# The input projection of a two-layer encoder as seven block products

## The chip, the cores and the metric

The kernel runs on one core of one Trainium2 chip. The time is device microseconds of one execution. Engines are named as in the profile: PE is TensorE's matmul (PEld its weight load), DVE is VectorE, ACT is ScalarE, POOL is GpSimd, SP is SyncE, which here only issues DMAs. Every row of a trace is from one execution.

## The reference

Two layers on 512 tokens of width 1024, all in float32. What one layer computes, cut to its core:

```python
h = rms_norm(x, g_pre_mix)
z = h @ w_in                      # 1024 x 6656
q, k, v, cb, cc, cx, ga, gb = split(z)   # 1024,256,256,1024,1024,1024,1024,1024
q, k = partial_rope(q), partial_rope(k)  # first 16 of 64 numbers of each head
y_attn = band_attention(q, k, v, sink) @ w_attn_proj   # |i-j| <= 128, 16 heads, 4 kv heads
y_conv = (cb * short_conv(cc * cx, conv_w)) @ w_conv_proj   # 3 taps
mix = (sigmoid(ga) * y_attn + sigmoid(gb) * y_conv) @ w_out
x = x + rms_norm(mix, g_post_mix)
h = rms_norm(x, g_pre_ffn)
x = x + rms_norm((silu(h @ w_gate) * (h @ w_up)) @ w_down, g_post_ffn)   # width 2816
```

## The kernel before

**Float32 from three products.** Every operand of a large matmul is kept as two parts: `h`, rounded to the matmul's format, and `lo`, the rest. ACT makes the first by a cast, DVE the second by a subtraction (`split_w` for weights, lines 129 to 131, and `split_to` for tokens, 205 to 207). A product is then three matmuls (`mm3`, lines 174 to 177): high times low, low times high, high times high, all into one PSUM bank.

**Stages of a layer.** (1) The norm, a transpose of the tokens by PE, and the value and key tiles. (2) The stretch with attention: a generator `products` yields the matmuls of the query tiles, of the conv's three column groups and of the conv projection, one k-block of three matmuls at a time, and pieces of attention (scores, softmax, transposed weights, values) are laid between them at even distances. (3) For each of eight column tiles the two gate products, their sigmoids, the attention projection and the merge. (4) `down` for `w_out`: all blocks but the last five first go through, the last five are kept in SBUF and finish the four token blocks one after the other, with the norms behind each. (5) The FFN's gate and up products. (6) `down` for `w_down`, six blocks kept.

In stages 1 to 3 the moving operand is the transposed tokens, 512 wide (256 for the keys), and a column tile of 128 takes 8 k-blocks of three matmuls.

**Stage 5 works by seven block products already.** `Rights` holds the token side: the 512 tokens and the 1024 rows form a 2 x 2 of blocks, and seven operands of 4 k-blocks by 256 tokens are made of them by sums and differences. `Pair` holds the weight side, two column tiles, one of the gate and one of the up matrix, as the other 2 x 2. Its `prep` makes the left operand of one product (a sum of blocks where needed, then the split), its `product` runs 12 matmuls of 256 columns and combines results on DVE. So a pair takes 7 x 12 matmuls of 256 columns. `orders` writes the order of the products by hand: five pairs open with products 2 and 1, which need the first 256 tokens alone, and later two pairs are in work at a time. Left operands are made five products ahead (`AHEAD`), loads begin ten ahead.

**What sets the order.** Every engine runs its own queue in order. The queues are filled by the framework's scheduler, which starts from the order of the code and moves instructions by its own estimate of when their inputs are there. Buffers: 22 units of 4 KB per partition (`u4`), six `t4`, six `t2`, eight `hl` (split weights), three `raw` (loaded weights); a tile waits until a buffer of its kind is free. Weight loads, stores of the layer's result and all other large DMAs are issued by SP.

**POOL** has little: the power -1/2 of the norms, two memsets per conv tile, and in the FFN one product of 256 columns per pair (line 448).

## Time and profile before

| | us |
|---|---|
| median of 3 runs | 1673.93 (1673.88 to 1674.6) |
| the profiled execution | 1674.66, its span 1672.9 |
| layer 0: start, values, keys | 0 to 39.6 |
| attention with query, conv products and conv projection | 39.6 to 314.3 |
| gates, attention projection, merge | 314.3 to 444.9 |
| `w_out` with norms | 444.9 to 489.0 |
| FFN products | 489.0 to 720.8 |
| `w_down` with norms | 720.8 to 838.0 |
| layer 1 and the end | 838.0 to 1672.9 |

A row of a group reads: line, engine, operation, what it writes and reads by the program's names, shapes and count, then busy microseconds, mean nanoseconds of one, and the idle time of the engine just before it with what ended it. A row of a timeline begins with start and duration. A row of a stretch (from:to) has its length and then, engine by engine, busy microseconds and in brackets the count. Busy PE time can hold matmuls that overlap, so the distance between starts is what a matmul costs.

### The profile page before, as it was taken

Reading aid. Unit: us, or ns where it says so; the run is one execution under the profiler, and the core shown is the slowest. Engines: PE = TensorE matmul, PEld = TensorE weight load, DVE = VectorE, ACT = ScalarE, POOL = GpSimd, SP = SyncE. Lnnn points to the kernel's source line nnn. Section 1 sums busy time; section 2 is a strip of 40 time slices with the busy share of each in tenths; the row PEclk is TensorE's granted clock in tenths of the full one; section 3 lists DMA queues with packets and bytes.
Section 4 is the critical chain, followed back from the end, with each engine's and each line's share of the span. In section 5 each row is a group of like instructions: output and inputs, shape, how many; then the busy total and the mean of one; then the engine's idle time right before and its main releaser. Section 6 shows DMA issues by size and latency. Waiting matters only on the chain.

```text
span 1672.9 us, 24896 instructions
## 1 busy us (share of the span) xinstructions
PE 1650.1 (99%) x9457; PEld 1454.9 (87%) x9457; DVE 1141.8 (68%) x2230; ACT 862.7 (52%) x1806; POOL 72.3 (4%) x114
## 2 busy tenths in 40 slices
PE   7999999999999999999999999999999999999998
PEld 7888888888889999988898888888888899999886
DVE  6988876434469988854469788754434899888442
ACT  5566666433346655543346666564333555556331
POOL 0000000000011100000000000000000011001000
PEclk9999999999999999999999999999999999999999
DMA  6322222433452333343413222224335333434332
GB/s 201 94 76 76 65 87 64 133 95 101 129 161 76 102 102 101 115 138 127 150 64 101 76 76 76 76 76 126 101 100 164 101 92 99 108 103 133 111 115 76
DMA packets 246937, 174.35 MB, mean 104 GB/s; under 512 B 5488, under 2 KB 232864, under 8 KB 246816
## 3 DMA queue, kind: packets, MB, share of 16 engines
q1 hardware_dynamic: 246096, 171.18, 34.6%
q8 instruction: 74, 1.21, 0.3%
q10 hardware_dynamic: 720, 1.57, 0.3%
q14 instruction: 47, 0.39, 0.1%
HBM read 164.34 MB, written 8.39 MB: 103 GB/s over the span
## 4 chain that ended last, share of the span: by engine, by line
PE 97%; DVE 2%; ACT 1%; DMA 0%; POOL 0%; issue 0%; POOLq 0%; DVEq 0%; ACTq 0%
PE bank L176 30%; PE bank L177 30%; PE bank L175 30%; PE bank L627 2%; PE bank L674 2%; PE bank L661 2%; PE bank L244 0%; DVE u L207 0%; DVE h L207 0%; DMA t<-in_x_dram 0%; ACT t L228 0%; PE bank L327 0%; DVE t L264 0%; POOL r L222 0%; DVE t L236 0%
## 5 line engine op out<-in xcount | busy, mean ns | idle before, releaser
L175 PE MATMUL bank<-h,hl 128*128 128x256 f32 (+1 forms) x1536 | 521.6, 340 | 1.1 <-DVE h L207 1.1
L176 PE MATMUL bank<-h,hl 128*128 128x256 f32 (+1 forms) x1536 | 518.2, 337 | 0.0
L177 PE MATMUL bank<-h,hl 128*128 128x256 f32 (+1 forms) x1536 | 517.8, 337 | 0.0
L131 DVE TENSOR_TENSOR hl<-raw,hl 128x512 fp32r<-128x512 f32 x428 | 292.8, 693 | 230.9 <-ACT hl L130 228.3
L130 ACT CAST hl<-raw 128x512 fp32r<-128x512 f32 x428 | 261.6, 620 | 323.4 <-PE bank L177 241.5
L177 PEld LDWEIGHTS bank<-h,hl 128*128 128x128 f32 x1536 | 292.2, 190 | 30.9
L175 PEld LDWEIGHTS bank<-h,hl 128*128 128x128 f32 x1536 | 292.5, 190 | 29.3 <-DVE h L207 1.9
L176 PEld LDWEIGHTS bank<-h,hl 128*128 128x128 f32 x1536 | 292.5, 190 | 27.6
L175 PE MATMUL bank<-u,hl 128*128 128x256 f32 (+1 forms) x784 | 251.2, 321 | 3.4 <-DVE u L207 3.4
L176 PE MATMUL bank<-u,hl 128*128 128x256 f32 (+1 forms) x784 | 250.2, 319 | 2.7 <-ACT u L206 1.8
L177 PE MATMUL bank<-u,hl 128*128 128x256 f32 (+1 forms) x784 | 250.0, 319 | 0.0
L175 PEld LDWEIGHTS bank<-u,hl 128*128 128x128 f32 x784 | 149.7, 191 | 13.8 <-DVE u L207 3.8
L176 PEld LDWEIGHTS bank<-u,hl 128*128 128x128 f32 x784 | 149.9, 191 | 13.0 <-ACT u L206 2.2
L177 PEld LDWEIGHTS bank<-u,hl 128*128 128x128 f32 x784 | 150.0, 191 | 10.3
L130 ACT CAST hl<-t 128x512 fp32r<-128x512 f32 x176 | 108.3, 621 | 58.2 <-DVE t L393 41.1
L131 DVE TENSOR_TENSOR hl<-t,hl 128x512 fp32r<-128x512 f32 x176 | 133.4, 765 | 6.0 <-ACT hl L130 3.9
L175 PE MATMUL bank<-hl,u 128*128 128x512 f32 x304 | 118.3, 389 | 0.0
L176 PE MATMUL bank<-hl,u 128*128 128x512 f32 x304 | 118.3, 389 | 0.0
L177 PE MATMUL bank<-hl,u 128*128 128x512 f32 x304 | 118.3, 389 | 0.0
L647 ACT ACTIVATE t<-t,neg 128x256 f32<-128x256 f32 (+1 forms) x128 | 70.4, 552 | 21.1 <-DVE neg L642 20.8
L632 DVE CUSTOM_DVE_ANT_0 t<-bank,tab,sink 128x256 f32<-128x256 f32 (+1 forms) x128 | 65.7, 541 | 6.1 <-PE bank L627 5.9
L448 POOL TENSOR_TENSOR u<-t 128x256 f32<-128x256 f32 x44 | 51.9, 1179 | 397.4 <-DVE t L444 236.6
(123 smaller groups left out, 2121.4 us busy)
## 6 DMA issues: line engine op xcount, KB each, us to landing
raw<-in_w_in_dram SPq DMA_DIRECT2D x104, 512.0 KB, 3.9
u<-in_w_up_dram SPq DMA_DIRECT2D x44, 512.0 KB, 5.9
raw<-in_w_down_dram SPq DMA_DIRECT2D x44, 512.0 KB, 3.5
raw<-in_w_gate_dram SPq DMA_DIRECT2D x40, 512.0 KB, 4.0
raw<-in_w_conv_proj_dram SPq DMA_DIRECT2D x16, 512.0 KB, 4.2
raw<-in_w_attn_proj_dram SPq DMA_DIRECT2D x16, 512.0 KB, 4.3
raw<-in_w_out_dram SPq DMA_DIRECT2D x16, 512.0 KB, 3.5
xd<-t SPq DMA_DIRECT2D x12, 512.0 KB, 2.9
```

The source lines that it names most:

```text
L130: nc.scalar.copy(h, raw)
L131: eng.tensor_tensor(out=lo, in0=raw, in1=h.bitcast(F32), op=ALU.subtract)
L175: nc.tensor.matmul(acc, wh, xl, start=first, stop=False, skip_group_check=goes_on)
L176: nc.tensor.matmul(acc, wl, xh, start=False, stop=False, skip_group_check=goes_on)
L177: nc.tensor.matmul(acc, wh, xh, start=False, stop=last, skip_group_check=goes_on)
L448: nc.gpsimd.tensor_tensor(out=out[:, TH:], in0=c22, in1=self.g[:, TH:], op=ALU.mult)
L627: nc.tensor.matmul(s[:, :w], q, kk[g][:, 1 - part, lo_b * P : lo_b * P + w], start=part == 0, stop=part == 1)
L632: nc.vector.tensor_tensor_reduce(out=p, in0=s[:, :w], in1=mask[:, m0 : m0 + w], scale=HD**-0.5, scalar=sink[:, h : h + 1], op0=ALU.add, op ...
L647: nc.scalar.activation(p, p, AF.Exp, bias=neg[:, i : i + 1], accum_out=den[:, i : i + 1])
L661: nc.tensor.transpose(pt[:, i * P : (i + 1) * P], p[:, n * P : (n + 1) * P], ident)
L674: nc.tensor.matmul(o, v, hl[:, 1 - part], start=n == 0 and part == 0, stop=kb == hi_b and part == 1)
```

## The change

**The input projection moves to `Pair`.** All columns but the values (50 tiles of a layer) become 25 pairs: one of keys, four of queries, eight of the conv (its X with its C columns), four of two B tiles each, eight of the two gates of one output tile. `orders` now also orders these, with four pairs opened early, and `products` yields them between the pieces of attention. The gate products move there from stage 3. Value tiles stay plain, with the tokens read from `Rights`; two of the four come after the transposes of the later tokens.

**A product's matmuls stand in another order:** for each k-block high times low and high times high, then all four low times high. Attention pieces can now stand between k-blocks of a product.

**More work on POOL.** `need` makes the two weight sums of a pair there, `rope` the sine product and the sum, the conv its product and the sum of two taps (the second tap's scaling goes to ACT), `Outer` the product with B, `sums` the token sums, the merge its gate product. In the FFN too the pair's two sums come from POOL, and DVE keeps two sums of four.

**DMA.** Rotated keys and queries are split whole and then moved to the two partition halves by DMAs (`move`), where ACT and DVE wrote the halves before. The conv results go to DRAM (`cyd`) and come back for the conv projection, the gates go to DRAM (`sgd`) and come back for the merge.

**Other edits.** Softmax by two heads instead of four, its scaling split evenly between ACT and DVE; attention's output kept in float32 and split behind the attention; units 22 to 20, `hl` 8 to 6, `t2` 6 to 8; separate buffers for scores; `down` keeps four blocks where it kept five and six; the next layer's first weights are loaded and split within `w_down`.

PE, where the products stand. Before, one k-block after another of 512 columns (`h` is the tokens, `hl` the split weights):

```order
L627 MATMUL bank_1405<-u_3_445,u_10_841 128x384 x2
L175 MATMUL bank_1364<-h_86,hl_1361 128x512
L176 MATMUL bank_1364<-h_86,hl_1361 128x512
L177 MATMUL bank_1364<-h_86,hl_1361 128x512
L175 MATMUL bank_1364<-h_86,hl_1361 128x512
L176 MATMUL bank_1364<-h_86,hl_1361 128x512
```

Of the change, one product:

```order
L421 MATMUL bank_1847<-h_95,hl_1780 128x256 x4
L417 MATMUL bank_1783<-h_95,hl_1811 128x256
L418 MATMUL bank_1783<-h_95,hl_1811 128x256
L417 MATMUL bank_1783<-h_95,hl_1811 128x256
L418 MATMUL bank_1783<-h_95,hl_1811 128x256
L417 MATMUL bank_1783<-h_95,hl_1811 128x256
L418 MATMUL bank_1783<-h_95,hl_1811 128x256
L417 MATMUL bank_1783<-h_95,hl_1811 128x256
L418 MATMUL bank_1783<-h_95,hl_1811 128x256
L421 MATMUL bank_1783<-h_95,hl_1811 128x256 x4
```

The tile's 24 matmuls of 512 columns became products of 12 matmuls of 256.

DVE, in the attention stretch of layer 0. Before (L131 is the split of a weight, L632 scores, L642 to L656 softmax, L207 the split of the transposed weights of attention, L606 of a query half):

```order
L650 TENSOR_TENSOR rd_2042<-den_2036,es_2034 128x4
L651 RECIPROCAL rd_2042<-rd_2042 128x4
L656 TENSOR_SCALAR t_43_1982<-t_43_1982,rd_2042 128x384
L656 TENSOR_SCALAR t_45_2023<-t_45_2023,rd_2042 128x384
L207 TENSOR_TENSOR t_46_2098<-bank_2093,t_46_2098 128x512
L606 TENSOR_TENSOR u_18_2058<-t_53_2052,u_18_2058 64x512 x2
L632 ISA t_47_2122,m_2121<-bank_2123,tab,sink 128x384
```

Of the change (L135 is the split of a weight, L397 a weight sum, L427, L433 and L446 combine products, L733 to L741 softmax, L204 the split for attention):

```order
L427 TENSOR_TENSOR t_33_2273<-bank_2216,t_33_2273 128x256
L733 TENSOR_TENSOR es_2247<-sink,neg_2246 128x2
L135 TENSOR_TENSOR hl_2293<-u_38_1889,hl_2293 128x512
L433 TENSOR_TENSOR t_30_2071<-bank_2137,t_30_2071 128x256
L135 TENSOR_TENSOR hl_2309<-raw_2151,hl_2309 128x512
L738 TENSOR_TENSOR rd_2249<-den_2248,es_2247 128x2
L446 SCALAR_TENSOR_TENSOR t_30_2071<-bank_2054,t_30_2071 128x256
L739 RECIPROCAL rd_2249<-rd_2249 128x2
L135 TENSOR_TENSOR hl_2325<-raw_2151,hl_2325 128x512
L741 TENSOR_SCALAR ps_2237<-ps_2237,rd_2249 128x384
L397 TENSOR_TENSOR t_42_2088<-t_42_2088,raw_1966 128x512
L204 TENSOR_TENSOR t_34_2342<-bank_2337,t_34_2342 128x512
```

Splits and combinations of the pairs now stand between the steps of attention.

POOL, in the same stretch. Before, memsets alone:

```order
L707 MEMSET t_40_1598 128x1
L708 MEMSET t_40_1598 128x1
L707 MEMSET t_47_1855 128x1
L708 MEMSET t_47_1855 128x1
L707 MEMSET t_58_2201 128x1
```

Of the change (L380 and L381 are weight sums, L587 and L591 the conv, L606 the product with B, L540 and L541 the rotation):

```order
L587 TENSOR_TENSOR t_39_2041<-t_25_1728 128x512
L380 TENSOR_TENSOR t_42_2088<-u_39_2086 128x512
L381 TENSOR_TENSOR u_39_2086<-u_39_2086,raw_1966 128x512
L591 TENSOR_TENSOR t_40_2045<-t_40_2045,t_41_2046 128x512
L606 TENSOR_TENSOR t_33_1662<-t_33_1662,t_27_1864 128x512
L380 TENSOR_TENSOR t_44_2290<-u_40_2288 128x512
L606 TENSOR_TENSOR t_40_2045<-t_40_2045,t_27_1864 128x512
L381 TENSOR_TENSOR u_40_2288<-u_40_2288,raw_2151 128x512
L380 TENSOR_TENSOR t_46_2490<-u_42_2488 128x512
L381 TENSOR_TENSOR u_42_2488<-u_42_2488,raw_2354 128x512
L540 TENSOR_TENSOR t_48_2510<-t_48_2510,tab 128x512
L541 TENSOR_TENSOR t_47_2509<-t_47_2509,t_48_2510 128x512
```

Sums, rotations and the conv's steps of 512 columns now follow each other in one queue.

The diff, cut to its core:

```diff
+UNITS, HL, T4, T2 = 20, 6, 6, 8
...
         def sums(self, t):
...
-            nc.vector.scalar_tensor_tensor(x22, x22, -1.0, x11, op0=ALU.mult, op1=ALU.subtract)
-            self.put(6, x22, cs)
+            nc.gpsimd.tensor_tensor(out=x11, in0=x22, in1=x11, op=ALU.add)
+            self.put(6, x11, cs, True)
             self.put(7, x12, cs)
-            nc.vector.scalar_tensor_tensor(x21, x22, -1.0, x21, op0=ALU.mult, op1=ALU.subtract)
+            nc.gpsimd.tensor_tensor(out=x21, in0=x11, in1=x21, op=ALU.subtract)
             self.put(4, x21, cs)
...
         def need(self, p):
...
+            if self.a1 is None:
+                l11, l21, l22 = self.raw[0][:, :512], self.raw[1][:, :512], self.raw[1][:, 512:]
+                self.a1 = t2([P, 512])
+                nc.gpsimd.tensor_tensor(out=self.a1, in0=l21, in1=l22, op=ALU.add)
+                nc.gpsimd.tensor_tensor(out=l21, in0=l21, in1=l11, op=ALU.add)
...
+            for k in range(KH):
+                nc.tensor.matmul(acc, hl[:, 0, k], lo[:, k], start=new and k == 0, stop=False, skip_group_check=not new)
+                nc.tensor.matmul(acc, hl[:, 0, k], h[:, k], start=False, stop=False, skip_group_check=not new)
+                yield HALF
+            for k in range(KH):
+                nc.tensor.matmul(acc, hl[:, 1, k], h[:, k], start=False, stop=k == KH - 1, skip_group_check=not new)
...
         def rope(acc):
...
-            nc.vector.tensor_tensor(out=r2, in0=r2, in1=sin, op=ALU.mult)
-            nc.vector.tensor_tensor(out=r1, in0=r1, in1=r2, op=ALU.add)
+            nc.gpsimd.tensor_tensor(out=r2, in0=r2, in1=sin, op=ALU.mult)
+            nc.gpsimd.tensor_tensor(out=r1, in0=r1, in1=r2, op=ALU.add)
+            hl = t4([P, 2, T], F32R)
+            split_to(hl[:, 0], hl[:, 1], r1)
...
+        def move(to, src):
+            nc.sync.dma_start(to.bitcast(F32), src.bitcast(F32))
...
+        class Conv(Pair):
+            def both(self):
...
+                nc.gpsimd.tensor_tensor(out=u[:, 1 : T + 1], in0=self.out0, in1=self.out1, op=ALU.mult)
...
+                nc.gpsimd.tensor_tensor(out=y, in0=y, in1=z, op=ALU.add)
...
+        class Outer(Pair):
...
+                    nc.gpsimd.tensor_tensor(out=ys[c], in0=ys[c], in1=acc, op=ALU.mult)
+                    nc.sync.dma_start(cyd[l][:, c], ys[c])
...
+        class Gates(Pair):
+            def both(self):
+                nc.sync.dma_start(sgd[l][:, self.m], self.v.rearrange("p a t -> p (a t)"))
...
+        order = [Keys(r, w_in, K0, w_in, K0 + P), queries(0), conv(0), queries(1), conv(1), outer(0)]
+        for n in (1, 2, 3):
+            order += [conv(2 * n), gates(2 * n - 2), conv(2 * n + 1), outer(n), gates(2 * n - 1)]
+            if n < 3:
+                order.append(queries(n + 1))
+        order += [gates(6), gates(7)]
...
         for m in range(KT):
-            acc = gemm(w_in, GB0 + m * P, xs)
...
-            acc = gemm(w_in, GA0 + m * P, xs)
...
+            sg = t4([P, 2, T])
+            nc.sync.dma_start(sg, sgd[l][:, m].rearrange("p (a t) -> p a t", a=2))
+            nc.scalar.activation(sg, sg, AF.Sigmoid)
+            nc.gpsimd.tensor_tensor(out=sg[:, 0], in0=sg[:, 0], in1=yc[m], op=ALU.mult)
+            acc = run(gemm_steps(a["w_attn_proj"][l], m * P, lambda k, part: at_hl[k][:, part]))
```

More of the change, by code (lines that the diff above doesn't have):

```diff
@@ L309, in __init__ @@
             self.x = {}
+            self.plain = plain
         def op(self, p):
@@ L760, in encoder @@
+                g = (ahead or at)["unit"][0]
+                pieces += [(g, first), (g, second)]
                 behind = (at, n)
[L761 to L764 removed]
+        pieces += [(0, []), (0, [lambda: values(*behind)])]
         steps = products()
[L766 to L770 removed]
+        total = (7 * len(order) * KH * HALF) + KT * KT * FULL
```

546 lines of the change are left out of this document (280 added, 266 removed).

## The prediction

> **What bounds the kernel now.** I read the page first: busy time by engine, then the chain that ended last.
>
> ```profile
> span 1672.9 us, 24896 instructions
> PE 1650.1 (99%) x9457; PEld 1454.9 (87%) x9457; DVE 1141.8 (68%) x2230; ACT 862.7 (52%) x1806; POOL 72.3 (4%) x114
> ...
> PE 97%; DVE 2%; ACT 1%; DMA 0%; POOL 0%; issue 0%; POOLq 0%; DVEq 0%; ACTq 0%
> ```
>
> TensorE (PE) is the bound nearly everywhere, so fewer PE microseconds are worth their whole length, as long as no other engine becomes longer than PE in the same stretch. Averages hide that, so the next view is busy time by stage: the input projection with attention and gates in layer 0 (39.6 to 444.9, of which 314.3 to 444.9 is the gate products and the attention projection), the FFN products (489.0 to 720.8), and its steady part.
>
> ```profile
> core 0: us, PE busy (x) PEld busy (x) DVE busy (x) ACT busy (x) POOL busy (x), PEclk, DMA share, GB/s
> 39.60:444.90 405.30, 405.30 (x1906) 337.83 (x1905) 264.21 (x595) 216.85 (x487) 1.07 (x16) 1.00 0.30 89
> ...
> 314.30:444.90 130.60, 130.60 (x577) 108.12 (x577) 51.74 (x78) 43.36 (x74) 0.00 (x0) 1.00 0.33 100
> ...
> 489.00:720.80 231.80, 228.21 (x1873) 226.49 (x1872) 210.34 (x361) 138.38 (x267) 27.17 (x24) 0.99 0.38 106
> ...
> 540.00:700.00 160.00, 160.00 (x1336) 160.00 (x1335) 142.68 (x243) 91.81 (x177) 19.16 (x16) 1.00 0.38 103
> ```
>
> PE never idles in the stretch to be changed (405.30 of 405.30), and VectorE (DVE) is busy 65% of it. In the FFN, which already works by seven products, DVE is busy 89%, and PE still does not wait. GpSimd (POOL) is empty in the first and lightly used in the second.
>
> **PE: what is saved.** Matmuls overlap in the trace, so their price is the pitch. 314.3 to 444.9 holds only 512-wide matmuls: 130.60 / 577 = 0.226 us each. The steady FFN holds only 256-wide ones: 160.00 / 1336 = 0.120, more than half of 0.226. The timeline of PE says the same, (703.94 - 699.74) / 35 = 0.120:
>
> ```profile
> 699.74 0.28 PE L175 MATMUL bank<-u,hl 128*128 128x256 f32 x1
> ...
> 703.94 0.28 PE L177 MATMUL bank<-u,hl 128*128 128x256 f32 x1
> ```
>
> A pair of column tiles costs 2 x 24 x 0.226 = 10.85 us plain, and 7 x 12 x 0.120 = 10.08 as seven products: 0.77 saved, 7% and not the eighth that the count of multiplications promises. Of 25 pairs in a layer, 24 were 512-wide; the key pair was done in halves, 96 x 0.120 = 11.52, and saves 1.44. That is 24 x 0.77 + 1.44 = 19.9 per layer; with the 0.227 that single pitches show it is 21. I take 21, so 42 for both layers. Value products and attention matmuls stay.
>
> **DVE: what is added.** Its price is also the distance from start to start. Two views of the FFN, DVE and then POOL, the second and third column being start and duration:
>
> ```profile
> 560.74 0.41 DVE L444 SCALAR_TENSOR_TENSOR t<-bank,t 128x256 f32<-128x256 f32 x1
> 561.07 0.68 DVE L393 TENSOR_TENSOR t<-t,raw 128x512 f32<-128x512 f32 x1
> 561.67 0.68 DVE L131 TENSOR_TENSOR hl<-t,hl 128x512 fp32r<-128x512 f32 x1
> 562.27 0.68 DVE L393 TENSOR_TENSOR t<-u 128x512 f32<-128x512 f32 x1
> ...
> 642.17 0.68 DVE L393 TENSOR_TENSOR t<-t,raw 128x512 f32<-128x512 f32 x1
> 642.77 1.23 DVE L131 TENSOR_TENSOR hl<-t,hl 128x512 fp32r<-128x512 f32 x1
> 643.92 0.68 DVE L393 TENSOR_TENSOR t<-u 128x512 f32<-128x512 f32 x1
> ```
>
> ```profile
> 561.29 4.67 POOL L448 TENSOR_TENSOR u<-t 128x256 f32<-128x256 f32 x1 [8.26 <-DVE t L444]
> ...
> 642.40 1.05 POOL L448 TENSOR_TENSOR u<-t 128x256 f32<-128x256 f32 x1 [10.28 <-ACT hl L130]
> ```
>
> A 512-wide DVE operation takes 0.60 back to back, a 256-wide one 0.33. And the two engines exclude each other: the DVE split that starts while POOL works (642.77) takes 1.23 instead of 0.68, and the POOL product at 561.29 needs 4.67 since DVE keeps coming first.
>
> In the 25-pair part of a layer DVE then has:
> - pairs: seven lo-splits and two sums at 0.60, three combinations at 0.33, 6.39 each, x25 = 159.8;
> - ten rotations, three DVE operations each (shuffle, cosine product, lo-split): 18;
> - eight conv taps: 4.8; sixteen token-operand splits and differences: 9.6;
> - attention, from the rows below: scores 32.9, prob splits 27.3, output sums 13.5, scaling 10.9, and small softmax operations, now by two heads instead of four: about 100 in pitches, of which about 85% falls beside the pairs, 85.
>
> ```profile
> L207 DVE TENSOR_TENSOR t<-bank,t 128x512 fp32r<-128x512 f32 x40 | 27.3, 682 | 7.6 <-ACT t L206 7.5
> L632 DVE CUSTOM_DVE_ANT_0 t<-bank,tab,sink 128x384 f32<-128x384 f32 x32 | 18.6, 608 | 0.3 <-PE bank L627 0.2
> L632 DVE CUSTOM_DVE_ANT_0 t<-bank,tab,sink 128x256 f32<-128x256 f32 x32 | 14.3, 475 | 2.7 <-PE bank L627 2.7
> ...
> L688 DVE TENSOR_TENSOR t<-bank,t 64x256 f32<-64x256 f32 x16 | 6.8, 428 | 8.3 <-ACT t L686 6.3 <-PE bank L627 1.6
> ...
> L689 DVE TENSOR_TENSOR t<-bank,t 64x256 f32<-64x256 f32 x16 | 6.7, 417 | 0.2
> ...
> L656 DVE TENSOR_SCALAR t<-t,rd 128x384 f32<-128x384 f32 x16 | 6.0, 418 | 0.3
> ...
> L656 DVE TENSOR_SCALAR t<-t,rd 128x256 f32<-128x256 f32 x16 | 4.9, 350 | 0.2
> ```
>
> Sum 277. PE has there 25 x 10.08 = 252, plus 6 for values, 2 for transposes and about 43 for attention: 303. DVE alone would fill 91% of it: just hidden.
>
> **POOL: the price that decides.** The part holds 98 POOL operations of 512 elements: 50 weight sums, 20 of the rotations, 16 of the conv, 8 outer products, 4 token sums. No such size is in the trace. The 256-wide one takes 0.739 undisturbed, and one element 0.549:
>
> ```profile
> L448 POOL TENSOR_TENSOR u<-t x44: 739/1052/4669, 522.3 to 1546.6; 128x256 f32<-128x256 f32 x44
> ...
> L222 POOL TENSOR_TENSOR r<-v,half x32: 549/550/555, 7.5 to 1667.9; 128x1 f32<-128x1 f32 x32
> ```
>
> With all of 0.549 as fixed cost, 512 take 0.549 + 2 x 0.190 = 0.93; with none fixed, 1.48. I take the middle, 1.2. What one costs DVE comes from the FFN's groups (22 POOL products fall in them), against 686 ns for the split where POOL is idle:
>
> ```profile
> L131 DVE TENSOR_TENSOR hl<-t,hl 128x512 fp32r<-128x512 f32 x88 | 66.4, 762 | 3.0 <-ACT hl L130 2.0
> L131 DVE TENSOR_TENSOR hl<-raw,hl 128x512 fp32r<-128x512 f32 x40 | 28.0, 701 | 7.6 <-ACT hl L130 6.8
> L393 DVE TENSOR_TENSOR t<-t,raw 128x512 f32<-128x512 f32 x40 | 27.2, 693 | 0.3
> ...
> L393 DVE TENSOR_TENSOR t<-u 128x512 f32<-128x512 f32 x22 | 16.5, 752 | 4.5 <-DMA u<-in_w_up_dram 4.5
> ...
> L131 DVE TENSOR_TENSOR hl<-raw,hl 128x512 fp32r<-128x512 f32 x81 | 54.7, 686 | 18.5 <-ACT hl L130 18.3
> ```
>
> (88 x 76 + 40 x 15 + 40 x 7 + 22 x 66) ns / 22 = 0.41 us lost per product. At 1.2 us the same share (0.41 / 0.739) gives 0.67, the same head start (0.33) gives 0.87; I take 0.75. In the new stretch more DVE operations read PSUM and can run beside POOL, but the queue is in order, so the next one waits. 98 x 0.75 = 74.
>
> In the Trainium skill, the page "SBUF — State Buffer", section "Who interferes with whom", makes this a lock: a VectorE instruction with two SBUF inputs and a GpSimd instruction that reads SBUF exclude each other for the whole instruction. The 1.23 and the 4.67 agree; its strict reading is the second rival below. "GPSIMD Engine Reference", section 3.1, gives 4497 ns for 2048 elements, from which with 0.739 I estimate 1.28 for 512; the sum by it would be 5 us more per layer.
>
> DVE also waits for ScalarE's (ACT) exponentials: in the waits of this stretch
>
> ```profile
> DVE rd L650 <- ACT es L648: 16.2, 12, 2.5
> ```
>
> in a layer; POOL can work during them, so I count half, 8. DVE then has 277 + 74 + 8 = 359 where PE has 303, and 56 us of PE idle per layer replace the 21 saved. ACT has less: 7 casts and 4 copies per pair, under 6 of 10 us.
>
> **The rest.** The FFN pair changes on DVE from 11 x 0.60 + 4 x 0.33 + 0.41 = 8.3 to 9 x 0.60 + 4 x 0.33 + 0.41 + 2 x 0.75 = 8.6 of 10.08: hidden behind PE, with two sums at 1.48 too. If that cover is gone, each further 0.1 us costs 4.4 over 44 pairs. Keeping four row blocks instead of five or six shortens the cover of the norm chain: between 0 and the 3.6 that the FFN row already shows as idle, three times; I take 3 in all. Spills, reloads and half-moves are DMA, whose share is 0.30: nothing, except as the third rival.
>
> Sum against the profiled execution's 1674.66: 1674.7 - 42 + 2 x 56 + 3 = 1747.7. That execution is 0.7 above the median of the three runs, so 1747.
>
> **Rivals.**
> 1. *POOL slips into DVE's gaps* (0.22): during operations that read PSUM, and waits. DVE has 303 - 277 = 26 us free and some 110 that need no second SBUF operand, against 98 x 1.2 = 118. Then PE stays the bound: 1674.7 - 42 + 3 - 0.7 = 1635, faster. Against it: all those FFN products cost DVE 0.41 on average.
> 2. *Every POOL operation blocks DVE for its length* (0.10): 277 + 98 x 1.2 + 8 = 403, 100 above PE: 1674.7 - 42 + 200 + 3 - 0.7 = 1835.
> 3. *The SyncE queue holds the weights back* (0.06): moves and spills wait there for late DVE results with weight loads behind. If each of the 20 rotated tiles of both layers costs a load's 3.9 to 4.0 us (page, `raw<-in_w_in_dram` row), 78 are lost: 1674.7 - 42 + 78 + 2 = 1713. For it: the moves stand among the loads. Against: loads are issued ten products ahead.
>
> ```profile
> raw<-in_w_in_dram SPq DMA_DIRECT2D x104, 512.0 KB, 3.9
> ```
>
> 4. *The saving is not made* (0.04): loss and gain meet within 0.2%, the least that a measurement of this kernel tells from no change.
>
> **How the numbers follow.** The forecast has 0.58. Its own range takes a POOL operation at 0.41 and no waiting (277 + 40 = 317, 14 over PE: 1663) to 1.1 and 16 of waiting (401: 1830). The range for 8 in 10 reaches down to the lower part of the gap before rival 1, and cuts the tail: 1640 to 1820. Faster: rival 1 and a sliver of the forecast, 0.23; same 0.04; slower 0.73.
>
> **What would show it.** Right: in the 25-pair part PE has idle time put down to DVE lo-splits, DVE is busy over 90%, POOL operations last 1.2 to 5 us, and DVE splits cluster at 0.68 and near 1.6; the FFN keeps its 10.08 us per pair; 84 products of a pair keep 0.120 where they run unbroken. Wrong: PE without idle there (rival 1), SyncE waits ending PE's (rival 3), or an FFN period over 10.1.

## Result and profile after

| | us |
|---|---|
| before, median of 4 | 1674.26 (1673.88 to 1674.6) |
| the change, median of 4 | 1853.4 (1851.47 to 1857.67) |
| ratio | 1.1074, 95% interval 1.1052 to 1.1095 |
| forecast | 1747 (1640 to 1820) |
| profiled execution of the change | 1855.02, span 1853.2 |

The change is slower, as forecast, but it loses 179 us where 73 were forecast, and its time lies above the forecast range. First the page of the change: engines, and PE, DVE and the granted clock in 40 slices.

```profile
span 1853.2 us, 29875 instructions
...
PE 1677.5 (91%) x11161; PEld 1548.0 (84%) x11161; DVE 1455.4 (79%) x2506; ACT 978.0 (53%) x2124; POOL 530.0 (29%) x422
...
PE   6779888899997999999987888888999989999998
...
DVE  7899999895658888872588999898956688888623
...
PEclk9899989999998999999998899898999989999999
```

PE was busy in 99% of the span; now it has holes, most of all in slices 0 to 7 and 20 to 27, the pairs of the two mixers (the stages of a layer up to `w_out`), where DVE is at 8 and 9 nearly throughout. The clock's digits dip here and there as well. By stretches (length, then busy time and count of PE, PEld, DVE, ACT and POOL, granted clock, DMA share, GB/s): most of the 25 pairs of layer 0, the rest of the mixer, the start and the steady part of the FFN; then layer 0's `w_down`, then layer 1's pairs.

```profile
33.00:418.90 385.90, 323.78 (x2388) 309.50 (x2386) 356.79 (x693) 226.92 (x550) 142.97 (x110) 0.93 0.37 102
418.90:514.70 95.80, 95.76 (x443) 79.55 (x444) 57.90 (x99) 51.77 (x94) 11.73 (x8) 1.00 0.51 154
556.00:630.00 74.00, 62.34 (x442) 59.62 (x441) 64.18 (x86) 37.11 (x75) 35.16 (x26) 0.88 0.26 72
630.00:790.00 160.00, 153.80 (x1255) 150.96 (x1254) 138.15 (x198) 80.75 (x165) 57.78 (x45) 1.00 0.37 100
...
811.70:934.80 123.10, 123.10 (x559) 102.10 (x558) 59.26 (x97) 50.70 (x96) 4.37 (x7) 1.00 0.46 138
...
934.80:1333.30 398.50, 338.37 (x2524) 324.49 (x2522) 363.24 (x708) 236.28 (x570) 149.83 (x116) 0.94 0.36 100
```

In the pairs' stretch of layer 0, which has 24 of the 25 pairs, DVE is busy 356.79 of 385.90, 92%. PE's 2388 matmuls need about 292 us at their undisturbed pitches: 2064 of 256 columns at 0.120, 66 of 512 at 0.226, and some 30 us for 258 short ones of attention. The length is DVE's work plus DVE's own waits: 356.79 + 29.1. In the steady FFN PE is short of its 160 too, by 6.2.

What ended PE's waits in the pairs' stretch (us in all, times, longest):

```profile
PE bank L763 <- DVE t L204: 20.3, 4, 8.3
PE bank L417 <- DVE t L446: 10.4, 11, 3.4
PE bank L417 <- DVE t L427: 10.2, 6, 3.8
PE bank L417 <- ACT hl L134: 6.4, 2, 4.6
PE bank L421 <- DVE hl L135: 4.7, 4, 2.2
```

Of the 62.1 us in which PE is idle there (385.90 - 323.78), some 47 end on DVE: at attention's split (L204), at the combinations of products (L446, L427) and, least of these, at the lo-splits of the weights (L135).

Where the 179 us came in can be read when both kernels are cut at the same matmuls. The table ahead of the prediction lets `w_down` run from 720.8 to 838.0, but these are its first and last matmul in layer 0, before and then in the change:

```profile
718.46 0.40 PE L175 MATMUL bank<-hl,u 128*128 128x512 f32 x1
841.34 0.39 PE L177 MATMUL bank<-u,u 128*128 128x512 f32 x1
...
811.68 0.40 PE L179 MATMUL bank<-hl,u 128*128 128x512 f32 x1
934.56 0.39 PE L181 MATMUL bank<-u,u 128*128 128x512 f32 x1
```

`w_down` has 528 matmuls of 512 columns in both kernels and takes 123.1 us in both. Stage lengths of the change less those of before, cut like this, layer 0 and layer 1: start to `w_out` +69.8 and +64.1; `w_out` and FFN (the FFN block) +23.5 and +22.9 (297.0 and 296.6 against 273.6 and 273.7); `w_down` and its norms 0 in both.

DVE next to POOL, from 253 to 259 us, as two timelines (start, duration), DVE first:

```profile
253.38 1.81 DVE L135 TENSOR_TENSOR hl<-t,hl 128x512 fp32r<-128x512 f32 x1
255.11 1.22 DVE L732 TENSOR_SCALAR neg<-m 128x2 f32<-128x2 f32 x1
256.24 0.68 DVE L397 TENSOR_TENSOR t<-t,raw 128x512 f32<-128x512 f32 x1
256.84 1.22 DVE L733 TENSOR_TENSOR es<-sink,neg 128x2 f32<-128x2 f32 x1
258.09 0.43 DVE L777 TENSOR_TENSOR u<-bank,t 64x256 f32<-64x256 f32 x1
...
260.89 0.14 DVE L738 TENSOR_TENSOR rd<-den,es 128x2 f32<-128x2 f32 x1
```

```profile
253.37 1.27 POOL L591 TENSOR_TENSOR t<-t,t 128x512 f32<-128x512 f32 x1 [0.87 <-ACT t L590]
254.59 1.72 POOL L381 TENSOR_TENSOR u<-u,raw 128x512 f32<-128x512 f32 x1
256.27 1.77 POOL L380 TENSOR_TENSOR t<-u 128x512 f32<-128x512 f32 x1
258.12 1.27 POOL L381 TENSOR_TENSOR u<-u,raw 128x512 f32<-128x512 f32 x1
```

The lo-split at 253.38 starts with POOL's sum and takes 1.81 instead of 0.68. The operations on 128x2 numbers at 255.11 and 256.84 take 1.22; their like at 260.89, with POOL quiet, takes 0.14. The 258.09 one reads PSUM and runs at its own 0.43 while POOL works. A POOL sum that nothing holds up takes 1.27.

### The profile page after: what moved, and what is told of

It is laid out like the page before. It is cut to its first block, busy times and chain, and to the rows that moved or that the text cites. A ratio compares the mean times of both kernels' runs of the same rounds, so it can differ in the third digit from the quotient of the medians.

```text
span 1853.2 us, 29875 instructions
## 1 busy us (share of the span) xinstructions
PE 1677.5 (91%) x11161; PEld 1548.0 (84%) x11161; DVE 1455.4 (79%) x2506; ACT 978.0 (53%) x2124; POOL 530.0 (29%) x422
## 5 line engine op out<-in xcount | busy, mean ns | idle before, releaser
L417 PE MATMUL bank<-h,hl 128*128 128x256 f32 x1504 | 390.0, 290 | 19.5 <-DVE h L204 9.4
L418 PE MATMUL bank<-h,hl 128*128 128x256 f32 x1504 | 385.4, 287 | 0.0
L417 PE MATMUL bank<-u,hl 128*128 128x256 f32 x1128 | 307.0, 301 | 74.9 <-DVE t L446 28.9
L135 DVE TENSOR_TENSOR hl<-raw,hl 128x512 fp32r<-128x512 f32 x328 | 238.4, 735 | 142.6 <-ACT hl L134 142.0
L135 DVE TENSOR_TENSOR hl<-t,hl 128x512 fp32r<-128x512 f32 x282 | 256.7, 911 | 78.2 <-ACT hl L134 75.4
L417 PEld LDWEIGHTS bank<-h,hl 128*128 128x128 f32 x1504 | 294.4, 196 | 23.2 <-ACT hl L134 11.1
L417 PEld LDWEIGHTS bank<-u,hl 128*128 128x128 f32 x1128 | 225.9, 200 | 92.7 <-DVE t L427 25.0
L418 PE MATMUL bank<-u,hl 128*128 128x256 f32 x1128 | 296.8, 292 | 0.0
L418 PEld LDWEIGHTS bank<-h,hl 128*128 128x128 f32 x1504 | 294.4, 196 | 0.0
L134 ACT CAST hl<-t 128x512 fp32r<-128x512 f32 x282 | 173.8, 618 | 214.3 <-DVE t L397 193.0
L134 ACT CAST hl<-raw 128x512 fp32r<-128x512 f32 x328 | 198.6, 620 | 156.0 <-PE bank L181 118.6
L421 PE MATMUL bank<-h,hl 128*128 128x256 f32 x1504 | 247.0, 287 | 3.0 <-DVE hl L135 2.9
L418 PEld LDWEIGHTS bank<-u,hl 128*128 128x128 f32 x1128 | 226.9, 201 | 0.0
L421 PEld LDWEIGHTS bank<-h,hl 128*128 128x128 f32 x1504 | 211.5, 195 | 4.7 <-DVE hl L135 4.5
L380 POOL TENSOR_TENSOR t<-u 128x512 f32<-128x512 f32 x94 | 149.9, 1596 | 205.3 <-DMA u<-in_w_in_dram 133.3
L421 PE MATMUL bank<-u,hl 128*128 128x256 f32 x1128 | 188.0, 290 | 6.3 <-DVE hl L135 6.3
L421 PEld LDWEIGHTS bank<-u,hl 128*128 128x128 f32 x1128 | 161.5, 199 | 8.4 <-DVE hl L135 8.2
L135 DVE TENSOR_TENSOR hl<-u,hl 128x512 fp32r<-128x512 f32 x200 | 166.3, 835 | 2.6 <-ACT hl L134 1.1
L397 DVE TENSOR_TENSOR t<-t,raw 128x512 f32<-128x512 f32 x176 | 160.0, 911 | 1.0
```

Source lines behind the costliest of these rows:

```text
L134: nc.scalar.copy(h, raw)
L135: eng.tensor_tensor(out=lo, in0=raw, in1=h.bitcast(F32), op=ALU.subtract)
L380: nc.gpsimd.tensor_tensor(out=self.a1, in0=l21, in1=l22, op=ALU.add)
L397: nc.vector.tensor_tensor(out=src, in0=src, in1=l11 if p == 6 else l12, op=ALU.add)
L417: nc.tensor.matmul(acc, hl[:, 0, k], lo[:, k], start=new and k == 0, stop=False, skip_group_check=not new)
L418: nc.tensor.matmul(acc, hl[:, 0, k], h[:, k], start=False, stop=False, skip_group_check=not new)
```

## Experiments

One core, each beside the kernel before (1674.2 to 1674.7 in every group). Experiments 1 to 4 are one execution each, the others four or five, which lay within 0.3% of each other. The theory after the result was that DVE sets the pace and that POOL's work is paid for by DVE. The rivals were an excess that has nothing to do with POOL's sums, late results, and the order or the transfers of the new stretch.

### 1. The weight sums out of POOL and DVE: 1742.4

The two tiles are set to zero by POOL; the sums are left out of the result.

```diff
-                nc.gpsimd.tensor_tensor(out=self.a1, in0=l21, in1=l22, op=ALU.add)
-                nc.gpsimd.tensor_tensor(out=l21, in0=l21, in1=l11, op=ALU.add)
+                nc.gpsimd.memset(self.a1, 0.0)
+                nc.gpsimd.memset(l21, 0.0)
```

> The two weight sums of each pair (50 in a layer's input projection, 44 in its FFN) become memsets of the same tiles on POOL: the sums are left out, the queue and its order stay, but POOL reads nothing for them. Theory (POOL's reads block DVE, 0.76 us per operation in the input projection and 0.71 in the FFN, as the trace of the change shows): the input projection loses 50 x 0.76 = 38 per layer, the FFN goes back towards its 232 (20 less per layer), so about 1853 - 116 = 1737, and DVE splits near 1.2 to 1.8 us become fewer by half. Rival (buffers, the order of the queues or waiting for POOL's results is what costs): the tiles are still written by POOL and still waited for, so the time stays within 20 us of 1853.

The kernel took 1742.39. The pairs' stretch of layer 0 fell from 385.9 to 351.9, the FFN block from 297.0 to 275.9, 2.3 more than before the change. So 111 of the 179 us hang on the 188 weight sums' reading and adding on POOL. DVE's number of instructions is unchanged. A memset is also done sooner than a sum (0.53 against 1.53 to 1.60 on average), so this run alone does not tell blocking from lateness.

### 2. The same sums on DVE: 1772.1

```diff
-                nc.gpsimd.tensor_tensor(out=self.a1, in0=l21, in1=l22, op=ALU.add)
-                nc.gpsimd.tensor_tensor(out=l21, in0=l21, in1=l11, op=ALU.add)
+                nc.vector.tensor_tensor(out=self.a1, in0=l21, in1=l22, op=ALU.add)
+                nc.vector.tensor_tensor(out=l21, in0=l21, in1=l11, op=ALU.add)
```

> The two weight sums of each pair go from POOL to DVE, in the input projection and in the FFN. Theory: a sum costs DVE 0.60 of its own where POOL's cost it 0.76 and 0.71, so 50 x 0.16 = 8 less per layer in the input projection and about 5 in the FFN, together about 1827; the FFN has DVE at 11 x 0.60 + 4 x 0.33 + 0.41 = 8.3 of 10.08 again. Rival (POOL relieves DVE and the lock is a small thing): 188 sums x 0.60 come onto an engine that is 92% busy in the input projection, 60 us more there, about 1910.

It took 1772.13, 81 us less than the change and less than expected. The engine said to be full took on 188 more operations, and its busy time fell from 1455.4 to 1396.5.

### 3. Everything of 512 columns on DVE: 1721.3

Rotations, conv sums, outer products, operand sums and weight sums; of ten such lines, two:

```diff
-            nc.gpsimd.tensor_tensor(out=r2, in0=r2, in1=sin, op=ALU.mult)
+            nc.vector.tensor_tensor(out=r2, in0=r2, in1=sin, op=ALU.mult)
...
-                nc.gpsimd.tensor_tensor(out=y, in0=y, in1=z, op=ALU.add)
+                nc.vector.tensor_tensor(out=y, in0=y, in1=z, op=ALU.add)
```

> All operations of 512 elements go from POOL to DVE: weight sums, rotations, conv, outer products, token sums, the gate product of the merge. Theory: 98 x 0.16 = 16 less per layer in the input projection and 5 in the FFN, about 1811; POOL's latency leaves the chains of rotation and conv, which takes a little more. No DVE operation of 512 elements is longer than 0.70 except beside the FFN's one POOL product. Rival (POOL relieves DVE): 98 x 0.60 = 59 more per layer, about 1970.

It took 1721.34, 90 less than the theory expected. Pairs of layer 0 and the block of `w_out` and FFN in this kernel:

```profile
33.00:370.90 337.90, 310.22 (x2395) 298.49 (x2394) 327.41 (x784) 224.98 (x550) 1.06 (x16) 0.98 0.42 116
464.60:743.70 279.10, 271.17 (x2062) 262.61 (x2061) 230.00 (x397) 153.81 (x306) 41.74 (x29) 0.99 0.42 119
```

DVE does 91 more instructions than in the change (784 against 693) and is busy 29 us less (327.41 against 356.79). So moving this work to POOL costs 132 us (1853.4 less 1721.3), 81 of them by the weight sums (experiment 2). But 47 us remain over the kernel before without any of it (19.7 and 15.8 in the mixers, 5.5 and 5.6 in the FFN blocks). In the pairs' stretch DVE is busy 327.41 of 337.90, 97%, where PE needs about 293.

### 4. Only the FFN's sums on DVE: 1832.5

```diff
+                eng = nc.vector if self.on_dve else nc.gpsimd
-                nc.gpsimd.tensor_tensor(out=self.a1, in0=l21, in1=l22, op=ALU.add)
+                eng.tensor_tensor(out=self.a1, in0=l21, in1=l22, op=ALU.add)
...
         class Gated(Pair):
+            on_dve = True
```

> Only the FFN's two weight sums go from POOL to DVE; the input projection stays as changed. Theory (POOL's sums cost the FFN its 20 us per layer): the stretch from w_out to w_down goes from 297 back to about 277, 1853 - 40 = 1813. Rival (fewer buffers, six split-weight tiles for eight and twenty units for twenty-two, and four kept blocks cost it): it stays at 290 or more and the time at 1840 to 1855.

It took 1832.45, between the theory and the rival: the FFN block falls to 284.5, by 12.5, and the pairs' stretch stays (384.8). The FFN's part of the loss is its own: 12.5 of the 23 us per layer go when its weight sums are done by DVE, and 21 when nobody does these (275.9 in experiment 1). Experiment 3, which within this block has only the four token sums on DVE besides, takes 279.1: four sums of POOL at the FFN's start cost another 5.4.

### 5. Only the FFN's sums on POOL, in the kernel before: 1736.7

```diff
+            if self.a1 is None:
+                l11, l21, l22 = self.raw[0][:, :512], self.raw[1][:, :512], self.raw[1][:, 512:]
+                self.a1 = t2([P, 512])
+                nc.gpsimd.tensor_tensor(out=self.a1, in0=l21, in1=l22, op=ALU.add)
+                nc.gpsimd.tensor_tensor(out=l21, in0=l21, in1=l11, op=ALU.add)
```

Beside these lines, DVE's two other sums of a pair are now formed in place in `a1`, as in the change, where the kernel before used two tiles in turn.

> The kernel before with one edit: the two weight sums a1 and l21 of each FFN pair on GpSimd, as in the change; nothing else differs. The prediction's FFN term, 8.6 us of DVE in 10.08 us of PE per pair, says 0: 1674. The run with the FFN's sums back on DVE, where an FFN block fell from 297.0 to 284.5, says 12.5 per layer even without the change's order, buffers and row blocks: about 1699.

The kernel took 1736.71 (1.0372, 1.0357 to 1.0388): 62 us, two and a half times the larger expectation, by the very part to which the prediction gave nothing. A steady part of its FFN, then DVE and POOL at one place of it:

```profile
540.00:720.00 180.00, 165.28 (x1326) 160.18 (x1325) 137.18 (x207) 86.59 (x178) 57.71 (x46) 1.00 0.31 83
```

```profile
621.29 1.24 DVE L131 TENSOR_TENSOR hl<-t,hl 128x512 fp32r<-128x512 f32 x1 [3.59 <-ACT hl L130]
622.56 1.66 DVE L403 TENSOR_TENSOR t<-t,raw 128x512 f32<-128x512 f32 x1
624.96 1.65 DVE L131 TENSOR_TENSOR hl<-t,hl 128x512 fp32r<-128x512 f32 x1 [0.74 <-ACT hl L130]
```

```profile
619.31 1.29 POOL L386 TENSOR_TENSOR t<-u 128x512 f32<-128x512 f32 x1 [9.39 <-DMA u<-in_w_up_dram]
620.68 1.29 POOL L387 TENSOR_TENSOR u<-u,raw 128x512 f32<-128x512 f32 x1
621.93 1.74 POOL L386 TENSOR_TENSOR t<-u 128x512 f32<-128x512 f32 x1
```

DVE is busy only 137.18 of 180, so it is not full. It stands 3.59 us at a split whose cast waits for POOL's sum, which POOL could begin only after 9.39 us without its load. All that is behind that split in DVE's queue stands too, among it the combinations that free PE's banks. In the 180 us casts wait 25.0 for POOL's first sum (`ACT hl L130 <- POOL t L386: 25.0, 7, 4.7`). A pair takes 180 / (1326 / 84) = 11.40 us.

### 6. The same with loads and sums asked for earlier: 1700.9

```diff
-            for j, q in seq[n : n + 2 * AHEAD]:
+            for j, q in seq[n : n + 4 * AHEAD]:
                 pairs[j].need(q)
```

> The kernel before with the FFN's weight sums on GpSimd (as in the run that took 1736.7), and loads and sums asked for twenty products ahead instead of ten; casts and splits stay at five. Theory, the sums come late (GpSimd waits up to 9.4 us for a load, works 2 x 1.3 to 1.7, and the cast and the lo-split behind it stand at the head of in-order queues): with twice the lead PE's idle 14.7 us of 180 goes, 1674 to 1690. Rival, the two engines' mutual exclusion is all of it: nothing changes, 1730 to 1740.

It took 1700.9 (1.0158, 1.0143 to 1.0174), between the two expectations. Its steady FFN:

```profile
540.00:700.00 160.00, 157.43 (x1302) 156.28 (x1301) 144.02 (x208) 87.29 (x175) 63.52 (x46) 1.00 0.37 97
```

A pair takes 160 / (1302 / 84) = 10.32 us, PE is nearly full again, and no cast waits for POOL's sums there. So 36 of the 62 us were lateness of loads and sums; the rest is left mostly at the FFN's start, where from 485 to 540 PE works on 317 matmuls and the kernel before on 393.

### 7. The same lead in the change: 1853.5

The edit of experiment 6, made in the change.

> The change, with block weights loaded and their two GpSimd sums asked for twenty products ahead instead of ten; nothing else. Theory, most of DVE's idle time in the pair stretch (29.1 of 385.9 us in layer 0, 8 forecast) is the split at the head of its queue waiting for a cast that waits for a late sum, and it falls by 14 to 20 per layer, the FFN blocks (297) by 8 to 13: 1790 to 1810. Rival, mutual exclusion and the rotations alone set the pace: 1840 or more.

It took 1853.48: no gain, the rival. Pairs of layer 0 and the block of `w_out` and FFN:

```profile
33.00:425.70 392.70, 327.25 (x2392) 315.88 (x2390) 346.42 (x695) 227.07 (x553) 138.21 (x109) 0.91 0.34 97
521.40:812.00 290.60, 276.87 (x2061) 266.49 (x2060) 239.52 (x349) 149.16 (x306) 92.43 (x77) 0.97 0.40 114
```

The FFN block gains 6.4 (297.0 to 290.6), the pairs lose 6.8, and DVE's idle time there grows from 29 to 46. Earlier sums of POOL do not cure the waits in the mixer. The waits of ACT say why: in the change's stretch casts wait 39.3 us for DVE's own sums (`ACT hl L134 <- DVE t L397: 39.3, 22, 5.4`) and 3.6 for POOL's (`ACT hl L134 <- POOL t L380: 3.6, 2, 1.8`); with the lead the wait for DVE's is 41.6.

### 8. The change without the lo-splits of the block weights: 1730.1

The third product of each block reads the high part again, times the tokens' low part; so the low part of these weights is left out of the result.

```diff
-            split_w(src, hl[:, 0], hl[:, 1])
+            nc.scalar.copy(hl[:, 0], src)
...
-                nc.tensor.matmul(acc, hl[:, 1, k], h[:, k], start=False, stop=k == KH - 1, skip_group_check=not new)
+                nc.tensor.matmul(acc, hl[:, 0, k], lo[:, k], start=False, stop=k == KH - 1, skip_group_check=not new)
```

> The change, with the lo-split of every block product's weights left out (the third twelve matmuls' weights are the high part once more, multiplied by the tokens' low part, so the low part of the weights is missing from the result); matmuls, order, GpSimd work, buffers and transfers stay. Theory, DVE's queue sets the pace in both stretches: DVE loses 175 splits x 0.60 = 105 us per layer of its 356.8 + 29.1, falls to about 281 under PE's 292, and PE is the bound again: 1674.7 - 42 plus at most 20 = 1633 to 1653. Rival, the order of products, the row blocks or the transfer queue hold PE: then the idle time stays, 1750 or more.

It took 1730.05 (1.0333, 1.0316 to 1.0350): 123 us of the 179 go, but the end is neither 1653 nor 1750.

```profile
33.00:368.60 335.60, 308.15 (x2384) 299.94 (x2383) 226.71 (x518) 226.36 (x548) 132.60 (x109) 0.96 0.43 116
```

DVE is busy 226.71 of 335.60, and PE still loses 44 on its 292. With DVE two-thirds busy something else holds PE; in the waits of this stretch ACT stands 26.6 us for the rotations' sums on POOL (`ACT t L203 <- POOL t L541: 26.6, 10, 3.7`: in all, times, longest).

### 9. Both: nothing on POOL, and no lo-splits: 1650.4

Experiments 3 and 8 in one kernel; the low part of the block weights is left out here as well.

> The change with all its 512-wide GpSimd operations on DVE and, as in the run that took 1730, the lo-split of the block products' weights left out (low part of the weights missing). DVE then has about 327 - 105 = 222 us of work beside PE's 293 and nothing waits for GpSimd. Theory, what held PE for 30 us per layer in the run without splits was waiting for GpSimd's late results: PE is the bound, 1633 to 1650. Rival, the order of products and the attention's chains hold PE whatever the engines: 1690 or more.

It took 1650.41 (0.9860, 0.9846 to 0.9875), as the theory expected.

```profile
33.00:336.50 303.50, 296.96 (x2377) 291.28 (x2376) 234.57 (x609) 224.95 (x545) 1.06 (x16) 0.99 0.47 129
432.20:704.60 272.40, 269.32 (x2061) 261.04 (x2060) 132.29 (x243) 155.72 (x306) 22.69 (x29) 0.99 0.43 122
```

PE is the bound again, with the change's order, buffers, spills, half-moves and four row blocks all in place: these do not hold it, which answers the SyncE rival of the prediction. DVE has 8 us more to do than in experiment 8, and the stretch is 32 us shorter: work on POOL costs more than the time that it takes from DVE, here by the waits for its results.

### 10 to 12. Only the gate pairs as seven products, at the start of the layer: 1707.2, 1697.7, 1705.6

To see whether the saving of 0.77 us per pair can be had with everything computed, the kernel before got only its eight gate pairs per layer as block products, all on DVE, with nothing new on POOL.

```diff
+    class Gates(Block):
+        def both(self):
+            nc.sync.dma_start(sgd[self.l][:, self.m], self.v.rearrange("p a t -> p (a t)"))
...
+        gate_products(l, w_in, hT)
         for n in range(2):
             run(query_tile(n))
```

> The kernel before, with only the eight gate pairs of each layer as seven block products, all sums on DVE, run at the start of the layer ahead of the queries (where DVE has 65% to do), spilled and merged as in the change; no rotation, conv or weight sum on GpSimd. Theory, the saving of 0.77 us per pair is real wherever DVE stays below PE (here 7.6 us of DVE per pair under 10.08): 16 x 0.77 = 12, less some 2 for the token operands: 1662 to 1664. Rival, forming the operands and the start of the products eat the saving, or the reload of the gates delays the merge: 1674 or more.

1707.18 (1.0194, 1.0179 to 1.0209), on the rival's side. From 80 to 140 us PE ran 502 matmuls in 60.0 us, 0.1195 each, without a gap. Ahead of that it stood 20.1 us for one cast, while DVE made the token operands. The clock was at half for 20.5 us, but most of that falls within the stand: PE worked only 3.5 us of it. In the next version four queries go ahead, with these operations spread among them:

```diff
-        for n in range(2):
-            run(query_tile(n))
+        parts = gr.make()
+        for n in range(NQ):
+            for i, _ in enumerate(query_tile(n)):
+                if i == 3 or n == 1 and i == 6:
+                    next(parts, None)
+        run(parts)
+        gate_products(l, w_in, gr)
```

> The gates-only kernel, with four queries instead of two ahead of the gate products (in place of none), and the eleven operations that form their token operands spread among these queries. Theory, its 33 us were the start: PE stood 20.1 us for one cast per layer while DVE made the operands, and then ran 20.5 us at half clock; behind 43 us of query products this is hidden and the saving shows: 1662 to 1670. Rival, seven products cost as much wherever they stand (late operands, late weights): 1690 or more.

1697.71 (1.0139, 1.0122 to 1.0156), 9.5 us better, but not hidden. Six queries, and one operation at a time:

> The gates-only kernel once more, now behind six queries, and the operations that form its token operands one by one, two to a query. In the run with four queries VectorE was busy 45.9 of 46.3 us there, and PE lost 11 us and then half of a 10.2 us spell. Six queries are 65 us of PE with 6 x 5.5 = 33 us of DVE, 11 us of keys and 15 us of operands: 59. Theory, the start is then hidden and the 12 us show: 1662 to 1668. Rival, the start stays DVE-bound, or products that attention loses to the front are missed there: 1680 or more.

1705.59 (1.0190, 1.0176 to 1.0204). The expected sum of 59 us under 65 was wrong as a cover: DVE was full up to 90 us (14.83 of 15.00 us just before it), and PE then lost time in small pieces up to 120. A DVE that is already full at the start of a layer (38 of 40 us from 40 to 80 in the kernel before) can't hide this work there, however it is spread.

### 13. The same pairs at the end of the mixer: 1669.0

The products stand where the plain gate products stood. Three attention projections go ahead and cover the making of the operands:

```diff
+        for m in range(NP):
+            st = gemm_steps(a["w_attn_proj"][l], m * P, lambda k, part: qs[k][:, part])
...
+                    next(st)
...
+                        next(parts, None)
...
+        run(parts)
+        gate_products(l, w_in, gr)
```

> The kernel before, with the eight gate pairs of each layer as seven products at the place where the plain gate products stood, at the end of the mixer, where DVE was busy 51.7 of 130.6 us; three of the eight attention projections go ahead of them and cover the making of the token operands, two or three operations per projection; everything on DVE, nothing left out. Theory, the saving of 0.77 us per pair needs only a DVE with room: 1674.2 - 12.3 plus 0 to 3 for the last attention results, which are now needed 80 us earlier: 1662 to 1665. Rival, seven products with their sums cost DVE and PE as much as they save wherever they stand: 1674 to 1700.

1669.0 against 1674.46: ratio 0.9964, interval 0.9950 to 0.9977, faster than both kernels, with nothing left out of the computation, but 4 us above what the theory allowed. Its gates, attention projection and merge:

```profile
313.00:440.00 127.00, 124.57 (x863) 116.38 (x862) 101.96 (x168) 67.04 (x126) 0.00 (x0) 1.00 0.55 175
```

DVE goes from 51.74 of 130.60 to 101.96 of 127.00, and PE stays the bound. Of the expected 12.3 us 5.5 came: the mixers gain 3.2 and 3.8 of 6.2 each, with 2.4 of PE idle here (127.00 - 124.57), and layer 1's FFN block is 1.5 longer.

## Why the prediction was half right

**The bound and the direction.** Right. DVE is busy 92% of the pairs' stretch, 47 of PE's 62 us of idle time end on it, splits stand at 0.68 and up to 1.81. But the sign that was named, PE idle put down to lo-splits of the weights, is the small part, 4.7; PE waits for what stands behind them in DVE's queue. And that 62 is near the 56 of the prediction is luck: the 56 were the stretch's length over PE's undisturbed need, and measured so they are 385.9 - 292 = 94. PE's busy time of 323.78 holds the rest, at a granted clock of 0.93.

**DVE's work, 277 + 74 = 351.** Right within a few per cent: 356.79 in layer 0 (24 of the 25 pairs), 363.24 in layer 1. The 0.75 that a POOL operation costs DVE was right in size: summing, over the like DVE instructions, what each took beyond the undisturbed duration of its kind gives about 77 us for 94 POOL operations (0.82 each) in layer 0, 74 for 98 (0.76) in layer 1 and 49 for 70 (0.71) in the FFN. So rivals 1 (nothing) and 2 (1.2 each) fall. But not only the splits paid. The groups of the change, line and form, busy time and mean:

```profile
L135 DVE TENSOR_TENSOR hl<-t,hl 128x512 fp32r<-128x512 f32 x282 | 256.7, 911 | 78.2 <-ACT hl L134 75.4 <-PE bank L421 0.8
...
L446 DVE SCALAR_TENSOR_TENSOR t<-bank,t 128x256 f32<-128x256 f32 x94 | 39.2, 417 | 5.6 <-PE bank L421 5.5
...
L738 DVE TENSOR_TENSOR rd<-den,es 128x2 f32<-128x2 f32 x64 | 32.0, 500 | 12.8 <-ACT es L737 12.8
L733 DVE TENSOR_TENSOR es<-sink,neg 128x2 f32<-128x2 f32 x64 | 31.3, 488 | 0.5
...
L732 DVE TENSOR_SCALAR neg<-m 128x2 f32<-128x2 f32 x64 | 25.9, 405 | 0.1
L741 DVE TENSOR_SCALAR ps<-ps,rd 128x256 f32<-128x256 f32 x32 | 19.9, 622 | 0.8
```

Splits of these sums lost about 0.23 each (911 against 686), but the small softmax operations, which the prediction had as pitches only, lost 0.25 to 0.34 each on 0.15 to 0.16 (their mean in experiment 9), and the scaling at L741 rose from 350 to 622. Combinations that read PSUM (L446, 417) lost nothing, as the prediction had it.

**DVE's waits, 8 per layer.** This is the step that failed in the mixer. They are 29.1 (385.90 - 356.79) and 35.3 (398.50 - 363.24). The prediction carried over half of one wait that the old trace shows, that for ACT's exponentials; it is 4.0 in this stretch of layer 0. The largest one is of splits that wait for their cast (`DVE hl L135 <- ACT hl L134: 12.3, 18, 1.6`), and the casts wait mostly for DVE's own sums (39.3, experiment 7). The chain sum, cast, split goes from DVE to ACT and back, and at the head of a queue in order such a split holds up all that is behind it. The waits hang on POOL: in layer 0's stretch they are 20.9 with the weight sums on DVE (experiment 2) and 10.5 with nothing of 512 columns on POOL (experiment 3). This mis-sizing, 21 and 27 us, is 48 of the 64 us by which the two mixers exceed the forecast (133.9 against 2 x 35); DVE's work over 351 (5.8 and 12.2) is of the size of the rest.

**The FFN, 0.** This step failed whole: 23 us per layer. DVE's work there came out as forecast. A pair's busy time goes from 142.68 / (1336 / 84) = 8.97 to 138.15 / (1255 / 84) = 9.25, +0.28 where +0.3 was forecast, still under the 10.08 of PE. Yet a pair takes 160 / (1255 / 84) = 10.71, over the 10.1 that the prediction named as a sign of being wrong. Comparing busy sums could not see it: in these 160 us DVE also stands 21.4 at splits whose casts are not done (`DVE hl L135 <- ACT hl L134: 21.4, 38, 0.8`), and 138.15 + 21.4 are 159.6. Work and waits together fill its queue. More than half of the loss lies at the FFN's start, where PE works on 442 matmuls from 556 to 630 and the kernel before on 556 from 486 to 560. The check that the prediction added, two sums at 1.48, gives 5.40 + 1.32 + 0.41 + 2.96 = 10.09 by its own prices, if a sum blocks DVE for its whole length, so that it was not hidden even there. Experiments 5 and 6 show in the kernel before that a late sum of POOL stops DVE's queue as well: 62 us, of which 36 go when loads and sums are asked for earlier. In the change the same lead gives 6.4 per FFN block, and there the casts of the steady part wait for DVE's own sums (`ACT hl L134 <- DVE t L397: 33.1, 15, 4.8`).

**PE's saving, 42.** Right in PE's work: with DVE relieved and POOL empty (experiment 9) PE is busy 19.8 and 19.0 us less per mixer (415.57 against 435.33, 411.10 against 430.10), where 21 were forecast. The mixers gain only 12.7 and 9.8 of it, since PE also idles 7 and 9 us more, and the kernel is 24 us under the one before. The pitch of 0.120 holds wherever the products run unbroken (experiment 10).

**The row blocks, 3.** They cost nothing that shows: `w_down` takes 123.1 us in layer 0 and 121.3 in layer 1 with four blocks kept as with six, and `w_out` 45.3 in both layers of both kernels.

**The sum.** 106 us above the forecast are 64 in the two mixers and 46 in the FFN blocks, less the 3 for the row blocks; the profiled executions differ by 1 us more than the medians. POOL operations take 1.27 undisturbed, not 1.2; the Trainium skill's page "GPSIMD Engine Reference", section 3.1, from which the prediction estimated 1.28, was nearer than the middle that it took.

**What stays open.** That POOL's operations and DVE's lo-splits together hold PE in the mixers is shown by experiment 9, and that the FFN pays for its sums on POOL by experiments 1 and 4. By which of POOL's results DVE's own waits grow is not isolated: the list of the change's stretch accounts for some 25 of 29 us, earlier weight sums do not cure them (experiment 7), and with these sums left out they are still 30.1 (experiment 1). Sums formed in place, fewer buffers and the new order may have a part in the 5.5 us per FFN block that remain in experiment 3; in experiment 10 sums in place on DVE did not hold PE (60.0 us without a gap). What the clock's dips cost is not measured either.

## To carry over

Before work is moved to GpSimd, price it by what it takes from VectorE's queue and not by GpSimd's free time: here moving 512-wide operations off a VectorE busy 97% of its stretch made it busier (327 to 357 us), and 132 us were lost. Where an engine's busy sum comes close to the bound's (here 9.25 of 10.08 us per pair), add the waits of its in-order queue from the chain sum, cast, split, and not only those that the old trace shows. A saving on the bound engine should be spent where the next engine has room: the same block products lost 23 to 33 us at the start of the layer and gained 5.5 at its end.

## What the runs showed of the hardware

**Operations of two numbers wait too.** DVE's 128x2 operations (L732, L733, L738) take 0.15 to 0.16 us on average with POOL quiet, and 0.99 to 1.21 where they overlap a reading operation of POOL, 19 to 22 of the 64 of each; `neg<-m` with its one input from SBUF (L732) is among them. What reads PSUM is not touched: L446 takes 0.417 apart from POOL and 0.414 beside it. In the Trainium skill, "SBUF — State Buffer", section "Who interferes with whom", the lock holds for instructions with two SBUF inputs or in a two-port mode, and no length is named as a condition; the trace agrees, with 1.22 on 128x2, and the prediction should have counted these by that rule. By the same section a POOL instruction that only writes doesn't contend with two-input ones. The trace of experiment 1 agrees: 85 lo-splits (L135) that overlap only a memset take 0.687 on average, those apart from POOL 0.685, and 117 beside a reading operation 1.126.

**The clock is halved without an idle window.** Four consecutive windows of the change (length 3.41 us, then as above; the clock is the number before the DMA share):

```profile
251.59:255.00 3.41, 1.11 (x10) 0.91 (x8) 3.41 (x6) 3.02 (x6) 2.54 (x3) 1.00 0.75 181
255.00:258.41 3.41, 0.00 (x0) 0.00 (x0) 3.38 (x5) 1.41 (x6) 3.33 (x3) 0.50 0.04 11
258.41:261.83 3.42, 0.81 (x2) 0.72 (x3) 3.39 (x8) 1.48 (x4) 1.05 (x3) 0.50 0.49 142
261.83:265.24 3.41, 3.41 (x17) 3.21 (x16) 3.41 (x8) 2.66 (x6) 0.00 (x0) 0.50 0.02 5
```

PE is busy 1.11 of 3.41 us, and the next window is granted half; half it stays until a window is full or nearly so. On this grid, all 23 windows at full clock after which the change's clock fell had PE busy 0 to 1.50 us; of the some 475 after which it stayed, one had 1.49 and all others 1.63 or more. A window at half clock that was followed by the full clock had 3.11 or more, one that was not 2.67 or less. The Trainium skill's page "TensorE: Matmul & The Clock Gate", Part 1, says an idle window halves the clock; here 1.5 us of work in it, 44%, did not prevent it. The spells are 55 of the 386 us in layer 0's stretch. DVE was idle 4% of the time in them and 8% outside (9% and 9% in layer 1), so nothing shows that they slow DVE, which sets the pace there; that they follow from its pace fits this and is not tested.
